# Turning the convolved values in 32x32 squares on VectorE, and one decay factor moved to POOL, in a hybrid DeltaNet and attention layer

## The chip, the cores and the metric

The kernel runs on one core of a Trainium2 chip. The metric is the device time in microseconds (us), the median of several executions. The engines are called as the profile calls them: PE (TensorE), DVE (VectorE), ACT (ScalarE), POOL (GpSimd) and SP (SyncE, whose queue issues most DMAs). PSUM holds what PE writes, SBUF is the on-chip memory, and tensors "spilled" go to device memory.

## What is computed

One layer over 2048 latent tokens and 256 context tokens of width 1024. Inputs are normed and modulated, then projected by `w_in`. Branch A is a gated DeltaNet of 4 heads, run forward and backward over the tokens; branch B is windowed attention. The part that matters here is the input of branch A:

```python
def _gdn_inputs(qkv_raw, beta_raw, decay_raw, conv_w, a_log, dt_bias):
    qkv = jax.nn.silu(_short_conv(qkv_raw, conv_w))          # 5 taps along the tokens
    q, k, v = jnp.split(qkv, [GDN_HEADS * GDN_DK, 2 * GDN_HEADS * GDN_DK], axis=-1)
    ...
    g = -jnp.exp(a_log) * jax.nn.softplus(decay_raw.reshape(b, l, 2, GDN_HEADS) + dt_bias)
# later, in chunks of tokens, for each direction:
gc = jnp.cumsum(to_chunks(g), axis=-1)
decay = jnp.where(incl, jnp.exp(jnp.where(incl, gc[..., :, None] - gc[..., None, :], 0.0)), 0.0)
```

So the values `v` of four heads (128 wide each) come out of a convolution along tokens and a SiLU, and a matrix of exponentiated decay differences is made for each 128 tokens, head and direction.

## The kernel before

The layer is worked in stages, and PE goes from one to the next without a break in the program: normed inputs and attention keys (to about 150 us), then the DeltaNet's values (`ORDER` 8 to 11, one head each), its keys (4 to 7), its queries (0 to 3), the gates, the chunk inverses, the scan over chunks, attention, and the output products.

`qkv` takes one head of one kind at a time. The tokens are cut into five segments: 256 of context and four of 512. For each segment `fm_dense` (L583 to L588) makes 24 matmuls into one of three PSUM buffers `lps`; ACT copies it to `y` (L696; four buffers); `conv` runs the five taps, the first on ACT (L623), four on DVE (L625), then a tanh on ACT (L626) and the closing product on DVE (L627). The result `cacc` has the head's 128 channels on the partitions and the tokens along the row. `finish` then puts it away. For values it was: PE transposes each 128 tokens into PSUM (L657, `zt`), ACT copies the four to `st` (L675), and one DMA stores `st`, tokens on the partitions, into `vsp` (L648, through `spill`), from where the scan loads it again (L1146).

Beside each of the first 18 segments runs one step of `all_decays`, the decay matrix of one 128-token chunk. `g` has been split into a high part `ghi` and a low part `glo`; for each direction and part, a tile `gm` = part times a 0/1 mask (`le` or `ge`) is made, and PE sums the four products of `gm` with a constant matrix in `dps` (L204). The four factors are made on different engines: number 0 (forward, high) on POOL, 1 (forward, low) and 2 (backward, high) on DVE, all by L202; 3 (backward, low) on ACT by four instructions (L200). ACT then takes the exponential (L207) and issues the store into `Dsp` itself.

Buffers matter in two places. The tile named `st` is a ring of two buffers, and factor 3 of the decays sits in the same ring; so within a head the ring is taken in this order: segment 0's `st`, `gm`, `gm`, segment 1's `st`, `gm`, segment 2's `st`, `gm`, segment 3's and segment 4's `st`, `gm`. Each taker waits until the one two before it is done with the buffer, for an `st` that means until its store has landed. Factors 0 and 1 share two buffers of their own. Values, keys and queries all use the ring `st`.

The order of instructions on every engine is set ahead of time by a scheduler that runs over a timeline of its own; each engine then runs its list strictly in order.

Of the kernel before, what the change touches and what calls it, by code (L numbers as in the profile page):

```python
# [7 lines left out]
F32 = mybir.dt.float32  # L8
# [12 lines left out]
H = 4  # L21
# [7 lines left out]
def f32(ap):  # L29
    return ap.bitcast(F32)  # L30
# [10 lines left out]
def _hybrid(ctx, tc, nc, V, S, G, T, ins, out, dbg, upto):  # L41
    dma = nc.sync.dma_start
# [5 lines left out]
    def dscr(name, shape, dt=F32):  # L48
        return dram.tile(shape, dt, name=name)
# [32 lines left out]
    g = pers.tile([128, NC, 8], F32, name="g")  # L82
# [9 lines left out]
    ksp = dscr("ksp", [NC, 128, H, 128])  # L92
    vsp = dscr("vsp", [NC, 128, H, 128])
# [49 lines left out]
    def psum(tag, shape, dt=F32, name=None):  # L143
        _, p, banks = pst["left" if tag in pst["left"][2] else "right"]
        return p.tile(shape, dt, name=name or tag, tag=tag, bufs=banks[tag])
# [44 lines left out]
    def decays(pool, matr, c, le, ge):  # L190


        dps = psum("gps", [128, H, 128], name="dps")
        n = 0
        for d, m in ((0, le), (1, ge)):
            for gx in (ghi, glo):
                gm = (pool.tile([128, H, 128], F32R, name="gm", bufs=2) if n < 2 else pb.tile([128, H, 128], F32R, name="gm", tag="dtl", bufs=1) if n == 2 else pb.tile([128, H, 128], F32R, name="gm", tag="st"))
                if n == 3:
                    for h in range(H):
                        S.activation(gm[:, h], m, AF.Copy, scale=f32(gx)[:, c, d * 4 + h:d * 4 + h + 1])  # L200
                else:
                    (G, V, V)[n].tensor_tensor(gm, f32(gx)[:, c, d * 4:d * 4 + 4].unsqueeze(2).to_broadcast([128, H, 128]),  # L202
                                               m.unsqueeze(1).to_broadcast([128, H, 128]), op=ALU.mult)
                T.matmul(dps, lhsT=matr[:, d], rhs=gm, start=n == 0, stop=n == 3)  # L204
                n += 1
        dt = pb.tile([128, H, 128], F32, name="dt", tag="o")
        S.activation(dt, dps, AF.Exp)  # L207
        adma(Dsp[c], dt)
# [41 lines left out]
    if True:  # L250
# [283 lines left out]
        for gi in range(8):  # L534
            xts = []
            for j in range(2):
                c = NCB + gi * 2 + j
# [13 lines left out]
            c = NCB + gi * 2  # L551
# [62 lines left out]
    pb = pb_.__enter__()  # L614
# [15 lines left out]
    def decay_of(h, c0, nn):  # L630
        dt = pb.tile([128, 4, 128], F32, name="dtl", bufs=1)[:, :nn]
        dma(dt, Dsp[c0:c0 + nn, :, h].rearrange("c p i -> p c i"))
        return dt

    def spill_blocks(d, t, c0, nn, h):

        for b in range(2):
            r = slice(b * 64, b * 64 + 64)
            dma(Nsp[d][c0:c0 + nn, h, b].rearrange("c r i -> r c i"), t[r, :, r])
        dma(offsp[d][c0:c0 + nn, :, h].rearrange("c r i -> r c i"), t[64:128, :, 0:64])  # L640

    def finish(m, z, c0, n):

        h = m % 4
        nn = n // 128
        b0 = c0 - NCB
        zc = [z[:, j * 128:(j + 1) * 128] for j in range(nn)]
        spill = lambda dst, t: dma(dst.rearrange("c p d -> p c d"), t)  # L648
        if m < 4:
            dma(qTsp[h, :, b0 * 128:b0 * 128 + n], z)  # L650
            kT = pb.tile([128, 4, 128], F32, name="kTl", tag="st")
            dma(kT, kTsp[h, :, c0 * 128:c0 * 128 + n].rearrange("p (c t) -> p c t", t=128))
        elif m < 8:
            dma(kTsp[h, :, c0 * 128:c0 * 128 + n], z)
        ps = psum("zt", [128, 4, 128])
        for j in range(nn):
            T.transpose(ps[:, j], zc[j], ident)  # L657
        if m < 8:
            dt = decay_of(h, c0, nn)
            for j in range(nn):  # L660
                junk = pb.tile([128, 128], BF16, name="junk", bufs=1)
                dst = ssk[:, c0 + j, h:h + 1] if m >= 4 else alpha[:, b0 + j, h:h + 1]
                S.activation(junk, ps[:, j], AF.Square, accum_out=dst)
            gps = psum("gps", [128, 4, 128])
            for j in range(nn):
                T.matmul(gps[:, j], lhsT=zc[j] if m >= 4 else kT[:, j], rhs=zc[j], start=True, stop=True)
            p = pb.tile([128, 4, 128], F32, name="p", tag="o")[:, :nn]
            V.tensor_tensor(p, gps[:, :nn], dt, op=ALU.mult)
            if m >= 4:
                spill_blocks(1, p, c0, nn, h)  # L670
            else:
                spill(QDsp[b0:b0 + nn][:, :, h], p)
        if m >= 4:
            st = pb.tile([128, 4, 128], F32, name="st")[:, :nn]
            S.copy(st, ps[:, :nn])  # L675
            spill((ksp if m < 8 else vsp)[c0:c0 + nn, :, h], st)
        if 4 <= m < 8:
            pps = psum("gps", [128, 4, 128])
            for j in range(nn):
                T.transpose(pps[:, j], p[:, j], ident)  # L680
            pt = pb.tile([128, 4, 128], F32, name="pt", tag="o")[:, :nn]
            S.copy(pt, pps[:, :nn])
            spill_blocks(0, pt, c0, nn, h)

    def qkv(order, after, w=None, beside=()):
        w = w or weights(w_in[:, order[0] * 128:order[0] * 128 + 128], KT)
        beside = iter(beside)
        for mi, m in enumerate(order):
# [3 lines left out]
            for si, (xh, xl, c0, n) in enumerate(segs):  # L692
                ps = acc([128, 512], name="lps")[:, :n]
                fm_dense(ps, w, xh, xl)
                y = py.tile([128, 516], F32, name="y", bufs=4)
                S.copy(y[:, 2:2 + n], ps)  # L696
                if c0 <= NCB:
                    V.memset(y[:, 0:2], 0.0)
                else:
                    V.tensor_copy(y[:, 0:2], ys[-1][0][:, 512:514])  # L700
                    V.tensor_copy(ys[-1][0][:, 514:516], y[:, 2:4])
                if c0 == 0 or c0 == NCB + 12:
                    V.memset(y[:, n + 2:n + 4], 0.0)
                ys.append((y, c0, n))
                if si == 1:
                    nxt = order[mi + 1] if mi + 1 < len(order) else after
                    wnext = None if nxt is None else weights(w_in[:, nxt * 128:nxt * 128 + 128], KT)
                if si == len(segs) - 1:
                    w = wnext
                    done = [ys[-2], ys[-1]]  # L710
                elif c0 > NCB or c0 == 0:
                    done = [ys[-1 if c0 == 0 else -2]]
                else:
                    done = []
                for y_, c_, n_ in done:
                    finish(m, conv(y_, m, n_), c_, n_)
                next(beside, None)
# [15 lines left out]
    def all_decays():  # L733
        matr = ev.tile([128, 4, 128], F32R, name="matr", tag="rt")[:, 0:2]
        V.tensor_copy(matr, mats[:, 2:4])
        scalars1()
        for c in range(NC):
            decays(dc, matr, c, le, ge)
            yield
# [942 lines left out]
```

## Time and profile before

| | us |
|---|---|
| median of 3 runs | 1963.31 (1960.19 to 1971.19) |
| the profiled execution | 1973.82 |
| its span, first to last instruction | 1972.1 |
| PE busy | 1910.1 |
| DVE busy | 1477.4 |
| ACT busy | 815.9 |
| POOL busy | 657.4 |

The profile is of one execution. PE, PEld (its weight loads), DVE, ACT and POOL are rows of busy time; an engine's list in order of time gives start, length and what it waited for just before. A group's row ends with "busy, mean ns of one | idle before, releaser".

### The profile page before, as it was taken

How to read it: one execution, taken by the hardware profiler on the slowest of the kernel's cores; microseconds unless marked ns; L12 is line 12 of the kernel's file. 1: busy time of each engine (PE TensorE's matmuls, PEld its weight loads, DVE VectorE, ACT ScalarE, POOL GpSimd, SP SyncE). 2: the span in 40 equal slices, each digit the busy share in tenths (PEclk: the TensorE clock that was granted, in tenths of full speed). 3: DMA queues.
4: the chain of work that ended last, by engine and by line, in shares of the span. 5: the costliest groups of instructions: out<-in, count | busy, mean ns of one | idle time of the engine just before them, and what ended most of it. 6: DMA issues, size and time to landing. Idle time of an engine off the chain costs nothing. (4 is left out here: it accounts for less than half of the span.)

```text
span 1972.1 us, 32045 instructions
## 1 busy us (share of the span) xinstructions
PE 1910.1 (97%) x10943; PEld 1606.0 (81%) x10943; DVE 1477.4 (75%) x2853; ACT 815.9 (41%) x2008; POOL 657.4 (33%) x750
## 2 busy tenths in 40 slices
PE   6899999989999999999999999999999999999999
PEld 3888888778998787887888888888878887878787
DVE  7889766677776999999778767544787777757864
ACT  6865545554444322211122233324675555532321
POOL 2652111235543201104222334422555444430353
PEclk9999999999999999999999999999999999999999
DMA  7553226765546633537887777755555555448362
GB/s 267 162 154 94 86 89 160 188 163 168 155 149 162 188 106 115 152 93 211 226 243 224 225 217 228 205 157 183 173 164 168 172 164 171 137 120 283 123 224 86
DMA packets 385463, 333.12 MB, mean 169 GB/s; under 512 B 83800, under 2 KB 307344, under 8 KB 384660
## 3 DMA queue, kind: packets, MB, share of 16 engines
q1 hardware_dynamic: 366292, 295.40, 51.7%
q10 hardware_dynamic: 19008, 35.67, 4.9%
q8 instruction: 87, 1.43, 0.3%
q14 instruction: 76, 0.62, 0.1%
HBM read 220.28 MB, written 109.13 MB: 167 GB/s over the span
## 5 line engine op out<-in xcount | busy, mean ns | idle before, releaser
L586 PE MATMUL rps<-hh,wh 128*128 128x512 f32 x768 | 309.8, 403 | 4.3 <-DVE rt L880 3.2
L587 PE MATMUL rps<-hl,wh 128*128 128x512 f32 x768 | 308.3, 401 | 0.0
L588 PE MATMUL rps<-hh,wl 128*128 128x512 f32 x768 | 307.2, 400 | 0.0
L625 DVE SCALAR_TENSOR_TENSOR cacc<-y,cw,cacc 128x512 f32<-128x512 f32 (+1 forms) x224 | 165.0, 758 | 21.1 <-ACT cacc L623 18.8
L586 PEld LDWEIGHTS rps<-hh,wh 128*128 128x128 f32 x768 | 145.4, 189 | 39.8 <-DVE rt L880 3.7
L588 PE MATMUL lps<-hh,wl 128*128 128x512 f32 (+1 forms) x448 | 171.7, 383 | 1.2 <-DVE wl L244 1.2
L586 PE MATMUL lps<-hh,wh 128*128 128x512 f32 (+1 forms) x448 | 172.0, 384 | 0.8 <-POOL wh L243 0.6
L588 PEld LDWEIGHTS rps<-hh,wl 128*128 128x128 f32 x768 | 145.3, 189 | 32.7
L587 PEld LDWEIGHTS rps<-hl,wh 128*128 128x128 f32 x768 | 145.7, 190 | 31.8
L587 PE MATMUL lps<-hl,wh 128*128 128x512 f32 (+1 forms) x448 | 171.0, 382 | 0.0
L1006 DVE TENSOR_TENSOR pl<-pt,ph 128x512 fp32r<-128x512 f32 x156 | 105.5, 685 | 45.8 <-ACT ph L1004 44.9
L1004 ACT CAST ph<-pt 128x512 fp32r<-128x512 f32 x156 | 90.6, 585 | 110.7 <-PE pt L1002 72.1
L878 ACT ACTIVATE rt<-rps 128x512 f32<-128x512 f32 x96 | 57.2, 596 | 185.1 <-PE rps L588 168.2
L978 DVE CUSTOM_DVE_ANT_0 pr<-sc,band,sk 128x640 f32<-128x640 f32 (+1 forms) x128 | 106.7, 862 | 19.9 <-PE sc L974 12.7
L811 DVE TENSOR_TENSOR N<-N,btmp 128x62 f32<-128x62 f32 (+30 forms) x124 | 118.1, 953 | 3.0
L988 POOL TENSOR_SCALAR pr<-pr,sm 128x640 f32<-128x640 f32 (+1 forms) x128 | 101.0, 809 | 55.8 <-DVE sm L986 40.3
L809 DVE TENSOR_TENSOR btmp<-N 128x62 f32<-128x62 f32 (+30 forms) x124 | 115.8, 934 | 3.1
L980 ACT ACTIVATE pr<-pr,sm 128x640 f32<-128x640 f32 (+1 forms) x128 | 104.0, 815 | 24.6 <-DVE sm L978 20.9
L244 DVE TENSOR_TENSOR wl<-wr,wh 128x512 fp32r<-128x512 f32 x120 | 90.8, 768 | 24.1 <-POOL wh L243 21.2
L1293 PE MATMUL pps<-yh,wph 128*128 128x512 f32 x256 | 105.7, 415 | 2.1 <-DVE tb L1304 2.0
L243 POOL TENSOR_SCALAR wh<-wr 128x512 fp32r<-128x512 f32 x72 | 50.3, 711 | 159.4 <-PE lps L587 57.2
L1295 PE MATMUL pps<-yh,wpl 128*128 128x512 f32 x256 | 101.9, 399 | 1.2 <-POOL wpl L1255 1.2
(396 smaller groups left out, 4961.4 us busy)
## 6 DMA issues: line engine op xcount, KB each, us to landing
wr<-in_w_in_dram SPq DMA_DIRECT2D x120, 256.0 KB
kw<-Ksp SPq DMA_DIRECT2D x28, 384.0 KB
x<-vsp SPq DMA_DIRECT2D x36, 256.0 KB
k<-ksp SPq DMA_DIRECT2D x34, 256.0 KB
kT<-kTsp SPq DMA_DIRECT2D x34, 256.0 KB
wm<-in_w_mod_dram SPq DMA_DIRECT2D x16, 512.0 KB
xt<-in_x_dram SPq DMA_DIRECT2D x16, 512.0 KB
dtl<-Dsp SPq DMA_DIRECT2D x32, 256.0 KB
```

The lines of the kernel that those rows point to most:

```text
L586: T.matmul(ps, lhsT=wh[:, k], rhs=xh[:, k], start=k == 0, stop=False)
L587: T.matmul(ps, lhsT=wh[:, k], rhs=xl[:, k], start=False, stop=False)
L588: T.matmul(ps, lhsT=wl[:, k], rhs=xh[:, k], start=False, stop=k == kt - 1)
L625: V.scalar_tensor_tensor(a, y[:, t:t + n], cw[:, m, t:t + 1], a, op0=ALU.mult, op1=ALU.add)
L809: V.tensor_tensor(tv, A[:, m + 1:, m].unsqueeze(2).to_broadcast([h1 + n, r, m]), A[:, m, 0:m].unsqueeze(1).to_broadcast([h1 + n, r, m]), o ...
L811: V.tensor_tensor(A[:, m + 1:, 0:m], A[:, m + 1:, 0:m], tv, op=ALU.add)
L978: V.tensor_tensor_reduce(s_, ps[:, o:768], band[:, b0:b0 + W + 256], -0.125, sk[:, 1, hd:hd + 1], ALU.add, ALU.min, sm[:, h, 1:2])
L980: S.activation(s_, s_, AF.Exp, scale=-1.0, bias=sm[:, h, 1:2], accum_out=sm[:, h, 2:3])
L988: G.tensor_scalar(p[:, h, :W + 256], p[:, h, :W + 256], sm[:, h, 3:4], 1.0, op0=ALU.mult, op1=ALU.mult)
L1006: V.tensor_tensor(pl, pt, f32(ph), op=ALU.subtract)
L1293: T.matmul(ps, lhsT=wh[:, k, ms], rhs=hs[k], start=k == 0, stop=False)
L1295: T.matmul(ps, lhsT=wl[:, k, ms], rhs=hs[k], start=False, stop=k == 3)
```

## The change

Two edits.

1. `finish` for values no longer uses PE, PSUM or ACT. DVE turns `cacc` by one instruction that transposes every 32x32 square in its place, straight into `st`. A partition of `st` then holds a token's place within 32, and the four groups of 32 partitions hold the four groups of 32 channels. Four DMAs, one for each group of partitions, put the squares where they belong in `vsp`, in runs of 32 numbers (128 bytes) where the one store of before had runs of 128 (512 bytes). What stands in `vsp` is the same.
2. Factor 1 of the decays (forward, low part) is made by POOL and not by DVE.

```diff
--- before.py
+++ after.py
@@ -199,7 +199,7 @@
                     for h in range(H):
                         S.activation(gm[:, h], m, AF.Copy, scale=f32(gx)[:, c, d * 4 + h:d * 4 + h + 1])
                 else:
-                    (G, V, V)[n].tensor_tensor(gm, f32(gx)[:, c, d * 4:d * 4 + 4].unsqueeze(2).to_broadcast([128, H, 128]),
+                    (G, G, V)[n].tensor_tensor(gm, f32(gx)[:, c, d * 4:d * 4 + 4].unsqueeze(2).to_broadcast([128, H, 128]),
                                                m.unsqueeze(1).to_broadcast([128, H, 128]), op=ALU.mult)
                 T.matmul(dps, lhsT=matr[:, d], rhs=gm, start=n == 0, stop=n == 3)
                 n += 1
@@ -652,6 +652,13 @@
             dma(kT, kTsp[h, :, c0 * 128:c0 * 128 + n].rearrange("p (c t) -> p c t", t=128))
         elif m < 8:
             dma(kTsp[h, :, c0 * 128:c0 * 128 + n], z)
+        if m >= 8:
+            st = pb.tile([128, 4, 128], F32, name="st")[:, :nn]
+            V.transpose(st, z.rearrange("p (c t) -> p c t", t=128))
+            for g in range(4):
+                dma(vsp[c0:c0 + nn, :, h, g * 32:g * 32 + 32].rearrange("c (k a) d -> a (c k) d", a=32),
+                    st[g * 32:g * 32 + 32].rearrange("a c (k d) -> a (c k) d", d=32))
+            return
         ps = psum("zt", [128, 4, 128])
         for j in range(nn):
             T.transpose(ps[:, j], zc[j], ident)
@@ -673,7 +680,7 @@
         if m >= 4:
             st = pb.tile([128, 4, 128], F32, name="st")[:, :nn]
             S.copy(st, ps[:, :nn])
-            spill((ksp if m < 8 else vsp)[c0:c0 + nn, :, h], st)
+            spill(ksp[c0:c0 + nn, :, h], st)
         if 4 <= m < 8:
             pps = psum("gps", [128, 4, 128])
             for j in range(nn):
```

Lines behind the new branch stand seven lines lower in the changed kernel (L675 is now L682, L696 is L703).

The scheduler sets a new order for everything from about the start of the values to the end of the queries; from the gates on the lists of the engines are the same as before. Three places show it. First PE, at the end of the context segment of a head (`zt` holds the turned values, `dps` the decay sums, `lps` the segment). Before:

```order
L586 MATMUL lps<-hh_412,wh 128x256
L587 MATMUL lps<-hl_413,wh 128x256
L588 MATMUL lps<-hh_412,wl 128x256
L657 MATMUL zt<-ident,cacc 128x128 x4
L204 MATMUL dps<-gm,matr 128x512
L586 MATMUL lps<-hh_412,wh 128x256
```

Now:

```order
L588 MATMUL lps<-hh_412,wl 128x256
L586 MATMUL lps<-hh_412,wh 128x256
L204 MATMUL dps<-gm,matr 128x512
L587 MATMUL lps<-hl_413,wh 128x256
L588 MATMUL lps<-hh_412,wl 128x256
```

The transposes are gone from the list in the values' part of the program; the matmuls of the decays stay, three together and one apart.

Second POOL, at the start of the values (`wh` is the high part of the next head's weights). Before:

```order
L243 TENSOR_SCALAR wh<-wr 128x512 x2
L202 TENSOR_TENSOR gm<-ghi,mats 128x512 x2
L243 TENSOR_SCALAR wh<-wr 128x512 x2
L202 TENSOR_TENSOR gm<-ghi,mats 128x512 x5
L243 TENSOR_SCALAR wh<-wr 128x512 x2
```

Now:

```order
L243 TENSOR_SCALAR wh<-wr 128x512 x2
L202 TENSOR_TENSOR gm<-ghi,mats 128x512
L202 TENSOR_TENSOR gm<-glo,mats 128x512
L202 TENSOR_TENSOR gm<-ghi,mats 128x512
L243 TENSOR_SCALAR wh<-wr 128x512 x2
L202 TENSOR_TENSOR gm<-glo,mats 128x512
L202 TENSOR_TENSOR gm<-ghi,mats 128x512
L202 TENSOR_TENSOR gm<-glo,mats 128x512
L202 TENSOR_TENSOR gm<-ghi,mats 128x512
L202 TENSOR_TENSOR gm<-glo,mats 128x512
```

Each decay step now has two products on POOL, the high and the low part of the forward direction; the weights' split stands between them.

Third, DVE in the middle of the second head, where the store of one segment's values and the transpose of the next meet in the ring. The list now has:

```order
L657 STREAM_TRANSPOSE st<-cacc 128x512
L705 MEMSET y 128x2
L625 SCALAR_TENSOR_TENSOR cacc<-y,cw,cacc 128x512 x2
L202 TENSOR_TENSOR gm<-ghi,mats 128x512
L625 SCALAR_TENSOR_TENSOR cacc<-y,cw,cacc 128x512
L657 STREAM_TRANSPOSE st<-cacc 128x512
L625 SCALAR_TENSOR_TENSOR cacc<-y,cw,cacc 128x512 x2
L627 SCALAR_TENSOR_TENSOR cacc<-y,cacc 128x512
L625 SCALAR_TENSOR_TENSOR cacc<-y,cw,cacc 128x512
L707 COPY y<-y 128x2
L625 SCALAR_TENSOR_TENSOR cacc<-y,cw,cacc 128x512
```

The first transpose is segment 1's and the next segment 2's. They use the same buffer, since the `gm` in between takes the other one; between them stand three convolution steps and one decay factor. DVE had no instruction on `st` before.

The queue of SP in the second to fourth head, before:

```order
L648 DMA vsp<-st 128x2x128
L239 DMA wr<-in_w_in_dram 128x4x128 x2
L648 DMA vsp<-st 128x4x128 x4
L239 DMA wr<-in_w_in_dram 128x4x128
L648 DMA vsp<-st 128x2x128
L239 DMA wr<-in_w_in_dram 128x4x128
L648 DMA vsp<-st 128x4x128 x4
L648 DMA vsp<-st 128x2x128
L239 DMA wr<-in_w_in_dram 128x4x128 x2
```

Now:

```order
L659 DMA vsp<-st 32x8x32 x4
L239 DMA wr<-in_w_in_dram 128x4x128 x2
L659 DMA vsp<-st 32x16x32 x16
L659 DMA vsp<-st 32x8x32 x4
L239 DMA wr<-in_w_in_dram 128x4x128 x2
L659 DMA vsp<-st 32x16x32 x16
L659 DMA vsp<-st 32x8x32 x4
L659 DMA vsp<-st 32x16x32 x4
L239 DMA wr<-in_w_in_dram 128x4x128 x2
L659 DMA vsp<-st 32x16x32 x4
```

Each store of before is four, in the same places among the loads of weights (`wr`).

## The prediction

> **What bounds the kernel now.** I read the page's busy row first, then the busy time by stretch, where the values are 150 to 290 us, the keys 290 to 440 and the queries 440 to 640 (columns: stretch and length; then busy us and instructions of PE, PEld, DVE, ACT and POOL; granted clock, DMA share, GB/s).
>
> ```profile
> PE 1910.1 (97%) x10943; PEld 1606.0 (81%) x10943; DVE 1477.4 (75%) x2853; ACT 815.9 (41%) x2008; POOL 657.4 (33%) x750
> 150.00:290.00 140.00, 140.00 (x698) 116.35 (x697) 111.47 (x195) 76.18 (x173) 28.88 (x28) 1.00 0.30 92
> 290.00:440.00 150.00, 141.50 (x854) 120.96 (x853) 100.28 (x203) 78.28 (x258) 31.64 (x31) 1.00 0.65 165
> 440.00:640.00 200.00, 198.56 (x1336) 179.16 (x1336) 145.82 (x333) 88.87 (x270) 90.61 (x105) 1.00 0.55 160
> ```
>
> The values stretch is the changed one, and there PE has no gap at all at full clock. DVE works 111.5 of 140 us, so 28.5 are free. What is taken from PE there shortens the stretch, one for one, as long as nothing else becomes late. In the keys and queries PE has 8.5 and 1.4 us of gaps.
>
> **The change on PE.** A stretch of PE's list shows what one set of transposes costs (start, length, instruction):
>
> ```profile
> 169.11 0.39 PE L586 MATMUL lps<-hh,wh 128*128 128x512 f32 x1
> 169.34 0.60 PE L657 MATMUL zt<-ident,cacc 128*128 128x128 f32 x4
> 169.70 0.48 PE L587 MATMUL lps<-hl,wh 128*128 128x512 f32 x1
> 170.02 0.39 PE L588 MATMUL lps<-hh,wl 128*128 128x512 f32 x1
> L657 PE MATMUL zt<-ident,cacc 128*128 128x128 f32 x72 | 11.1, 272 | 0.0
> ```
>
> Matmuls overlap, so starts count, not lengths. Two 512-wide matmuls in a row start 0.23 apart (169.11 to 169.34). From the four transposes' start to that of L588 there are 0.68 us, where one matmul alone would need 0.23: four transposes cost 0.45. In all there are 72 in the values (last row, the group of this stretch): 18 sets of four would be **8.1 us**. Nothing is put on PE. The decays' 72 matmuls stay.
>
> **ACT** loses its 20 copies (L675, 10.8 us, and the waits ahead of them). It is not the bound, but the waits stood in front of first taps that DVE needs:
>
> ```profile
> L675 ACT COPY st<-zt 128x512 f32<-128x512 f32 (+1 forms) x20 | 10.8, 542 | 21.7 <-PE zt L657 20.3 <-DMA vsp<-st 1.5
> DVE cacc L625 <- ACT cacc L623: 15.2, 6, 4.9
> ```
>
> ACT sat 20.3 us waiting for the transposes, and DVE in its turn sat 15.2 us waiting for ACT's first tap, up to 4.9 at once. Of DVE's idle time this is over half, and it should shrink. It gives DVE room; it gives the end nothing by itself, since PE has no gap there.
>
> **The change on DVE.** Three rows of DVE and one of POOL in the values stretch:
>
> ```profile
> L202 DVE TENSOR_TENSOR gm<-glo,mats 128x512 fp32r<-128x512 f32 x18 | 17.0, 944 | 8.1 <-PE dps L204 8.1
> L202 DVE TENSOR_TENSOR gm<-ghi,mats 128x512 fp32r<-128x512 f32 x18 | 12.3, 682 | 0.2 <-PE dps L204 0.2
> L625 DVE SCALAR_TENSOR_TENSOR cacc<-y,cw,cacc 128x512 f32<-128x512 f32 x68 | 53.7, 825 | 9.6 <-ACT cacc L623 9.1
> L202 POOL TENSOR_TENSOR gm<-ghi,mats 128x512 fp32r<-128x512 f32 x18 | 20.9, 1162 | 80.2 <-PE dps L204 68.9 <-DMA Ksp<-ks 11.3
> ```
>
> Moved away: 18 factors of 0.68 undisturbed (the `ghi` row), 12.3 us. Added: 16 transposes of 128x512 and 4 of 128x256. The trace has no such instruction. From below I bound it by one pass over 512 numbers, the `ghi` row's 0.68, from above by two passes, 1.36. I take one (half for the small ones), since the two 512-wide rows here, of different operations, lie close together: 16 x 0.68 + 4 x 0.34 = 12.2, and at most 24.5. So DVE's own work stays as it is, -0.1 us, or grows by 12.
>
> POOL gets 18 more products. It has room (28.9 of 140 us), but it disturbs DVE:
>
> ```profile
> 161.42 0.68 DVE L202 TENSOR_TENSOR gm<-ghi,mats 128x512 fp32r<-128x512 f32 x1
> 162.05 1.50 DVE L625 SCALAR_TENSOR_TENSOR cacc<-y,cw,cacc 128x512 f32<-128x512 f32 x1
> 161.85 1.16 POOL L202 TENSOR_TENSOR gm<-ghi,mats 128x512 fp32r<-128x512 f32 x1 [0.89 <-PE dps L204]
> 167.28 0.68 DVE L202 TENSOR_TENSOR gm<-ghi,mats 128x512 fp32r<-128x512 f32 x1
> 167.89 1.51 DVE L625 SCALAR_TENSOR_TENSOR cacc<-y,cw,cacc 128x512 f32<-128x512 f32 x1
> 169.44 0.75 DVE L625 SCALAR_TENSOR_TENSOR cacc<-y,cw,cacc 128x512 f32<-128x512 f32 x1
> 167.50 1.35 POOL L202 TENSOR_TENSOR gm<-ghi,mats 128x512 fp32r<-128x512 f32 x1 [4.50 <-PE dps L204]
> ```
>
> A convolution step takes 0.75 alone and 1.50 while POOL makes a factor, 0.76 more. Over the stretch the loss is less, for some of POOL's work falls into DVE's gaps: the `glo` factors lie 0.262 x 18 = 4.7 us above the `ghi` ones, the 68 steps 0.075 x 68 = 5.1 above 0.75; 9.8 us for POOL's 28 instructions in these two groups, 0.35 each, and with the smaller groups about 0.5, my estimate. Eighteen more: 9 us; at the least 0, at the most 18 x 1.16 = 20.9.
>
> The Trainium skill, "SBUF — State Buffer", section "Who interferes with whom", says that a DVE instruction with two inputs in SBUF and a GpSimd instruction that reads SBUF exclude each other, the later one waiting for the whole of the earlier. The two pairs above agree in kind; the stretch's mean is less. [...] The transpose has one input and by that section would not be stopped.
>
> **The stores and the ring.** Each store becomes four. What an issue, a landing and a packet cost:
>
> ```profile
> L648 SPq DMA_DIRECT2D vsp<-st x20: 359/360/458, 154.5 to 283.9; - x20
> L1058 SPq DMA_DIRECT2D x<-X4sp x32: 573/610/1251, 1212.3 to 1271.5; - x32
> 182.25 0.59 ACT L675 COPY st<-zt 128x512 f32<-128x512 f32 x1 [0.76 <-PE zt L657]
> 185.85 0.38 ACT L675 COPY st<-zt 128x256 f32<-128x256 f32 x1 [0.55 <-DMA vsp<-st]
> DMA packets 417, 0.21 MB, mean 103 GB/s; under 512 B 16, under 2 KB 417, under 8 KB 417
> q1 hardware_dynamic: 417, 0.21, 38.2%
> DMA packets 207, 0.05 MB, mean 49 GB/s; under 512 B 207, under 2 KB 207, under 8 KB 207
> q1 hardware_dynamic: 207, 0.05, 26.3%
> DMA packets 376, 0.02 MB, mean 23 GB/s; under 512 B 376, under 2 KB 376, under 8 KB 376
> q1 hardware_dynamic: 376, 0.02, 22.7%
> ```
>
> The old store was done 3.0 us after the copy (182.84 to 185.85). The packet rows are three short windows: 512-byte stores of `vsp` in 2 us (0.382 x 16 x 2 / 417 = 29 ns each), 256-byte stores of `Nsp` in 1 us (20 ns), 64-byte loads of `X4sp` in 1 us (10 ns). Between them a 128-byte packet is about 13 ns; at worst as much as a 512-byte one, 29. A set of four stores has 2048 packets: 1.7 us on 16 engines (3.7 at worst) where 512 took 1.0. DMA is at a share of 0.30 here, so room is not the matter; the landing is. Issues of patterns cut like these cost 0.61 (`X4sp` row), plain ones 0.36: the fourth goes out 1.1 to 1.8 us later than one alone, which gives 4.1 to 4.8 us behind the transpose if the packets keep up; where packets are slower than the issues it is 3.0 - 1.0 + their time, 5.7 at 29 ns. I take 4.5, between 4.1 and 6.
>
> Behind the stores on SP wait the loads of weights, at most two us longer. They are early by far more: POOL, which splits them, waits for PE to free the buffers, not for the load. The same list of waits has POOL early with the decays too, by 68.9 / 17 = 4.1 us a step, so a second product of 1.16 fits before PE needs it.
>
> ```profile
> POOL gm L202 <- PE dps L204: 68.9, 17, 8.5
> POOL wh L243 <- PE lps L587: 34.1, 5, 20.2
> ```
>
> The Trainium skill, "DMA: Bandwidth & Descriptors", section "Specifications", puts line rate at 512 bytes and more, with a read-modify-write below. The 256-byte row shows no such step (20 ns against 29), but no run here shows 128-byte stores.
>
> Now DVE waits where ACT did: a transpose waits for the store that last held its buffer, and the convolution steps behind it on DVE wait too, then `y`, the `lps` buffers and PE. I went through DVE's new list at 0.67 a step (162.05's neighbours start so), 0.6 for other 512-wide ones, half for 256, and added 0.5 to 0.7 for POOL. Between two transposes of one buffer there are, head by head, about 5.2, 4.6 and 4.3 us in the first, 3.1, 5.2 and 2.8 in the second, 3.1, 5.2 and 3.6 in the third, 4.4 and 3.5 in the last. At 4.5 us the waits add up to 1.4 + 1.7 + 1.4 + 0.9 + 1.0 and some tenths, near 7 us; at 6 us to 21; below 3 to almost nothing.
>
> **The sum.** DVE: 111.5 - 0.1 + 9 + 7 = 127 us. PE: 140 - 8.1 = 131.9. DVE still fits, but at 96%, and PE waits in order for factor 2 of the decays, which stands behind those waits on DVE. I give back 3 of the 8.1. The keys and queries have a new order with the same work; I leave their 9.9 us of gaps as they are. So -5 us: the profiled execution, 1973.82 (its span 1972.1 and 1.7 around), would be 1968.8. It lies 10.5 above the median of the runs, 1963.3, which becomes **1958 us**; this case's own range is 1954 to 1963. A measurement of this kernel tells 0.5%, 9.8 us, from no change.
>
> **Rivals.**
>
> *DVE takes PE's place.* POOL's added products stop DVE for all of their length: 111.5 - 0.1 + 20.9 = 132.3 before any wait for the ring. PE is then paced by DVE, the 8.1 are given back: 1961 to 1967, 1964. For it: the two pairs above. Against it: the mean over the stretch, and the part of DVE's 15.2 us that goes with ACT's copies. The page on SBUF has the rule.
>
> *Slower: the stores hold the ring.* If a set of four lands 7 us after the transpose and not 4.5, the gaps above leave 21 + 11 = 32 us of waits on DVE, 111.5 + 9 + 32 = 152.5 against 140: 12.5 longer, 1976. It decides from 6 us on, where the gain is gone (111.5 + 9 + 21 = 141.5). For it: four issues, four times the packets, and a DVE that stands still in order. Against it: 7 us need packets of 39 ns (3.0 - 1.0 + 2048 x 0.039 / 16), above every row. The page on DMA has the rule that could do it.
>
> *Gain on both sides.* The reordered keys also lose gaps. They had 8.5, of which 6.1 stood ahead of L680:
>
> ```profile
> L680 PE MATMUL gps<-ident,p 128*128 128x128 f32 x72 | 11.4, 277 | 6.1 <-DVE p L668 2.5 <-DVE y L698 2.1 <-DVE y L700 0.7
> ```
>
> With all 8.1 and half of these gone it is -11 to -12: 1952. For it: those waits are questions of order on DVE, which enters the keys with less behind it. Against it: nothing in the diff touches the keys, and order can add as well.
>
> **How the numbers follow.** Forecast 0.50, DVE in PE's place 0.20, slower by the ring 0.14, gain on both sides 0.16. Faster by over 0.5% (below 1953.5) is the last case and a little of the first, 0.18; slower (above 1973.1) is the ring and a little of an unlucky order, 0.16; the same 0.66. For 8 in 10 the range takes the first two cases whole and reaches into the other two: 1949 to 1971.
>
> **What would show it.** In the changed profile: L657 gone from PE and STREAM_TRANSPOSE on DVE, near 0.68 (1.36 makes DVE the bound); PE in the values without gaps ahead of L204 and L586, the stretch some 5 us shorter; L625's mean above 825 ns, by how much tells POOL's price; "DVE st waited for DMA vsp" near 7 us in the waits, and 20 or more if the ring rival holds; `glo` on POOL at 1.0 to 1.2. The prediction is wrong if the stretch is not shorter, or if the gaps of the keys move by more than a few us.

## The result

The change made the kernel slower. The changed kernel's median is 1977.02 us (1972.09 to 1980.12), against 1965.47 us (1960.19 to 1971.19) for the kernel before in the same comparison: time after / time before is **1.0054**, 95% interval 1.0041 to 1.0066. A second comparison (in the next section) gave 1.0034, 1.0017 to 1.0050 (1973.96 against 1966.81 us). One lies above the 0.5% that I had called the limit of a measurement and one below, but neither interval holds 1. The forecast was 1958, and the range ended at 1971.

The profiled execution of the changed kernel has a span of 1970.4 us and is the shortest of its seven runs, while the one of before (1972.1) is longer than all of its own; the two spans must not be subtracted. What can be compared is how far each has come at the same point of the program. I take ACT's copies of the 56 segments out of PSUM into `y` (20 of values, 20 of keys, 16 of queries). The fourth, the twentieth and the last in the list of ACT before (start, length, instruction, idle before):

```profile
152.96 0.59 ACT L696 COPY y<-lps 128x512 f32<-128x512 f32 x1 [1.55 <-PE lps L588]
...
255.26 0.57 ACT L696 COPY y<-lps 128x512 f32<-128x512 f32 x1
...
610.22 0.58 ACT L696 COPY y<-lps 128x512 f32<-128x512 f32 x1
```

And after:

```profile
152.71 0.59 ACT L703 COPY y<-lps 128x512 f32<-128x512 f32 x1 [0.89 <-PE lps L588]
...
262.30 0.57 ACT L703 COPY y<-lps 128x512 f32<-128x512 f32 x1
...
615.43 0.58 ACT L703 COPY y<-lps 128x512 f32<-128x512 f32 x1
```

From the fourth to the twentieth copy, that is in the values, it was 102.3 us and now is 109.6: **7.3 us lost where 5 were to be gained**. From the twentieth to the last, keys and queries, it was 355.0 and now is 353.1. The loss is in the stretch that the change touches; some 1.6 of the 7.3 us are matmuls that only moved there (4 more of the decays and 6 more half-wide ones between the two copies, at 0.23 and 0.12 us a start), so that from the fourth copy to the last it is 5.5 us.

The stretches of the changed kernel (columns as in the prediction) say that PE, which had no gap from 150 to 290 us, now has 10.8 us of them and a granted clock of 0.98:

```profile
150.00:290.00 140.00, 129.21 (x586) 104.47 (x585) 122.87 (x201) 68.11 (x161) 51.10 (x44) 0.98 0.40 92
290.00:440.00 150.00, 142.35 (x853) 122.39 (x853) 96.78 (x196) 76.80 (x258) 33.59 (x35) 1.00 0.67 171
440.00:640.00 200.00, 199.67 (x1357) 181.01 (x1356) 143.95 (x331) 87.10 (x258) 89.37 (x103) 1.00 0.51 153
```

Its list of waits for 150 to 290 us (engine, tile, line, what it waited for: total, times, longest) names what PE, DVE and ACT stood for:

```profile
ACT cacc L623 <- DVE st L657: 24.9, 14, 3.2
...
ACT gm L200 <- DMA vsp<-st: 11.2, 7, 2.8
PE dps L204 <- DVE gm L202: 8.6, 7, 2.6
DVE st L657 <- DMA vsp<-st: 7.4, 9, 1.5
...
DVE cacc L625 <- ACT cacc L623: 4.3, 9, 0.8
...
PE dps L204 <- DVE y L710: 2.2, 1, 2.2
```

PE's 10.8 us stand ahead of L204, the decays' matmuls. They wait for factor 2 (backward, high), the one that DVE still makes, and once for an entry behind it in DVE's list. DVE comes to factor 2 late: transposes ahead of it wait for the ring, and convolution steps are stretched while POOL works. Ahead of the longest gap (2.6 us, from 229.2) the ring took only 0.7 us of DVE's time since 215, but three pairs of steps took 2.2 to 2.35 us each, where one alone takes 0.75. ACT waits twice: its factor 3 for a store that leaves the ring (11.2 us, 6.5 before), and, new, its first tap for a transpose that still holds the `cacc` buffer (24.9). The groups of DVE and POOL in the same stretch:

```profile
L625 DVE SCALAR_TENSOR_TENSOR cacc<-y,cw,cacc 128x512 f32<-128x512 f32 x72 | 65.5, 912 | 5.3 <-ACT cacc L623 4.3
...
L202 POOL TENSOR_TENSOR gm<-glo,mats 128x512 fp32r<-128x512 f32 x18 | 21.8, 1209 | 28.0 <-PE dps L204 28.0
...
L202 DVE TENSOR_TENSOR gm<-ghi,mats 128x512 fp32r<-128x512 f32 x18 | 13.9, 774 | 0.0
...
L657 DVE STREAM_TRANSPOSE st<-cacc 128x512 f32<-128x512 f32 x16 | 11.3, 706 | 6.4 <-DMA vsp<-st 6.4
...
L657 DVE STREAM_TRANSPOSE st<-cacc 128x256 f32<-128x256 f32 x4 | 1.8, 443 | 1.0 <-DMA vsp<-st 1.0
```

A convolution step costs 912 ns in place of 825, a transpose 706 (443 at half width).

The gaps cost more than their length. Three neighbouring slices of 4 us:

```profile
226.00:230.00 4.00, 3.20 (x23) 2.67 (x22) 3.72 (x5) 0.27 (x2) 2.31 (x2) 1.00 0.00 0
230.00:234.00 4.00, 2.20 (x5) 1.81 (x6) 3.22 (x8) 1.71 (x4) 0.00 (x0) 0.70 0.28 82
234.00:238.00 4.00, 4.00 (x16) 3.14 (x16) 3.53 (x4) 2.32 (x7) 1.22 (x1) 0.87 1.02 248
```

Behind PE's longest gap the granted clock is 0.70 and 0.87. Over the 35 slices of the stretch, PE's busy time times what is missing to 1.00 comes to 2.8 us. Gaps and clock together are 13.6 us; 8.1 off that leaves +5.5, as much as from the fourth copy to the last.

### The profile page after: what moved, and what is told of

The parts are those of the page before. It is cut to its first block, busy times and chain, and to the rows that moved or that the text cites. A ratio compares the mean times of both kernels' runs of the same rounds, so it can differ in the third digit from the quotient of the medians.

```text
span 1970.4 us, 31964 instructions
## 1 busy us (share of the span) xinstructions
PE 1897.6 (96%) x10871; PEld 1594.1 (81%) x10871; DVE 1487.5 (75%) x2855; ACT 806.6 (41%) x1988; POOL 681.3 (35%) x768
## 5 line engine op out<-in xcount | busy, mean ns | idle before, releaser
L625 DVE SCALAR_TENSOR_TENSOR cacc<-y,cw,cacc 128x512 f32<-128x512 f32 (+1 forms) x224 | 172.6, 781 | 8.5 <-ACT cacc L623 5.6
L985 DVE CUSTOM_DVE_ANT_0 pr<-sc,band,sk 128x640 f32<-128x640 f32 (+1 forms) x128 | 106.7, 862 | 19.9 <-PE sc L981 12.2
L244 DVE TENSOR_TENSOR wl<-wr,wh 128x512 fp32r<-128x512 f32 x120 | 93.7, 792 | 27.6 <-POOL wh L243 24.8
L1301 PE MATMUL pps<-yl,wph 128*128 128x512 f32 x256 | 101.6, 398 | 0.0
```

Source lines behind the costliest of these rows:

```text
L625: V.scalar_tensor_tensor(a, y[:, t:t + n], cw[:, m, t:t + 1], a, op0=ALU.mult, op1=ALU.add)
L985: V.tensor_tensor_reduce(s_, ps[:, o:768], band[:, b0:b0 + W + 256], -0.125, sk[:, 1, hd:hd + 1], ALU.add, ALU.min, sm[:, h, 1:2])
L1301: T.matmul(ps, lhsT=wh[:, k, ms], rhs=ls[k], start=False, stop=False)
```

## The experiments

My theory after the result: PE loses in the values what it waits for factor 2, and DVE is late there by three things that add up: its own work, POOL's disturbance, and the ring of two `st` buffers. Rivals: POOL's disturbance alone, the stores alone, the new order of the lists alone, or something in the later stages. Where the text speaks of "gaps + clock", it is as just worked out, for 150 to 290 us; "4 to 20" and "20 to 56" are the times between these copies into `y`, "tail" the time from the last one to the end of the span.

| kernel | time / time before (95%) | gaps + clock | 4 to 20 | 20 to 56 | tail |
|---|---|---|---|---|---|
| before, first profile | | 0.0 + 0.0 | 102.3 | 355.0 | 1361.9 |
| before again | 0.9992 (0.9979 to 1.0006) | 0.0 + 0.0 | 102.3 | 353.2 | 1353.4 |
| changed, first profile | 1.0054 (1.0041 to 1.0066) | 10.8 + 2.8 | 109.6 | 353.1 | 1355.0 |
| changed again | 1.0034 (1.0017 to 1.0050) | 12.4 + 2.6 | 111.9 | 354.7 | 1357.2 |
| transposes alone | 1.0007 (0.9993 to 1.0022) | 5.4 + 1.4 | 106.5 | 350.8 | 1359.2 |
| factor 1 to POOL alone | 1.0006 (0.9994 to 1.0019) | 0.7 + 0.0 | 104.0 | 353.9 | 1363.4 |
| changed, own buffer for factor 3 | 0.9991 (0.9978 to 1.0003) | 2.9 + 0.0 | 99.7 | 350.3 | 1360.7 |
| changed, factor 2 on POOL too | 1.0050 (1.0034 to 1.0066) | 11.2 + 0.0 | 113.3 | 349.6 | 1353.0 |
| changed, one plain store | 1.0003 (0.9988 to 1.0018) | 6.5 + 3.0 | 108.7 | 344.7 | 1350.8 |
| transposes, own buffer | 0.9958 (0.9941 to 0.9974) | 1.9 + 0.0 | 97.7 | 349.0 | 1352.1 |
| the same again | 0.9959 (0.9942 to 0.9975) | 1.9 + 0.0 | 97.7 | 351.9 | 1352.0 |
| before, own buffer | 0.9991 (0.9977 to 1.0005) | 0.0 + 0.0 | 104.2 | 349.9 | 1356.6 |
| transposes, own buffer, factor 2 on ACT | 0.9945 (0.9930 to 0.9960) | 0.0 + 0.0 | 95.6 | 350.1 | 1351.8 |
| the same, factor 1 on POOL | 0.9970 (0.9959 to 0.9982) | 0.0 + 0.0 | 96.8 | 351.5 | 1353.9 |

The tail runs over the same lists in all of them and still varies by 12 us from one profiled execution to the next (8.5 between the two of the kernel before). So the times of whole kernels are taken from the ratios, and the profiles are used for the stretch. ACT copies some segments a few us late, which "4 to 20" and "20 to 56" trade against each other. And every edit lets the scheduler set a new order from the values to the queries, so no run differs from another in its edit alone; what an edit is worth is the edit together with the order that came with it.

**Both kernels again.** No edit.

> The kernel before once more, for a second profile beside the first and for the noise of the comparison. All theories: ratio 1.000 within 0.3%, median 1960 to 1970 us; PE without a gap from 150 to 290 us (140.0 of 140).

> The changed kernel once more, for a second profile. Its first profile (1972.1) is the lowest of its seven runs and loses only some 5 us by the end of the queries. Theory (PE waits in the values for factor 2 of the decays, which stands on DVE behind convolution steps, transposes and their waits; what PE saved goes into these waits and into the slower clock after them): ratio 1.004 to 1.007, about 10 us of gaps on PE ahead of L204 again and a granted clock below 1.00 behind them. Rival (the loss is in the keys and queries, by their new order alone): the values as long as or shorter than before, the keys and queries together longer by 5 us or more. Rival (the loss is in the later stages, by the clock): the gates start no later than before and the loss comes after 700 us.

Before against itself is 0.9992, so 0.15% either way is what such a comparison leaves open. The changed kernel is slower again, and by the table again in the values (9.6 us), not in the keys and queries (1.5 more than before again, 0.3 less than its first profile) and not in the tail. From the fourth copy to the last it takes 11.1 us more than before again, where gaps and clock less 8.1 make 6.9, so that account is a rough one. Its ratio lies just under the 1.004 that the theory gave as the least. The rival of later stages falls, and that of a new order in the keys and queries; the order within the values is not told apart here. Here is one wait in full. DVE in the second profile of the changed kernel, at the end of a head:

```profile
180.31 2.93 DVE L625 SCALAR_TENSOR_TENSOR cacc<-y,cw,cacc 128x256 f32<-128x256 f32 x4
183.15 0.16 DVE L708 COPY y<-y 128x2 f32<-128x2 f32 x1
183.22 0.16 DVE L707 COPY y<-y 128x2 f32<-128x2 f32 x1
185.22 0.71 DVE L657 STREAM_TRANSPOSE st<-cacc 128x512 f32<-128x512 f32 x1 [1.83 <-DMA vsp<-st]
185.85 0.38 DVE L627 SCALAR_TENSOR_TENSOR cacc<-y,cacc 128x256 f32<-128x256 f32 x1
186.16 0.68 DVE L202 TENSOR_TENSOR gm<-ghi,mats 128x512 fp32r<-128x512 f32 x1
```

and PE at that time:

```profile
184.12 0.40 PE L204 MATMUL dps<-gm,matr 128*128 128x512 f32 x1
186.89 0.79 PE L204 MATMUL dps<-gm,matr 128*128 128x512 f32 x1 [2.37 <-DVE gm L202]
187.49 0.63 PE L587 MATMUL lps<-hl,wh 128*128 128x512 f32 x1
187.91 0.63 PE L588 MATMUL lps<-hh,wl 128*128 128x512 f32 x1
188.34 0.63 PE L586 MATMUL lps<-hh,wh 128*128 128x512 f32 x1
```

The transpose stands 1.83 us for the store of an earlier one; factor 2, two places behind it, is late by that; PE waits 2.37 us with its next matmuls of `lps` ready, and then starts a matmul every 0.43 us in place of 0.23 for the next 2.5 us (187.49 to 189.99).

**Transposes alone**, factor 1 stays on DVE:

```diff
-(G, G, V)[n].tensor_tensor(gm, ...
+(G, V, V)[n].tensor_tensor(gm, ...
```

> Transposes on DVE and four stores as in the change, but factor 1 stays on DVE. DVE then has 111.5 + 11.3 = 122.8 us of work in the values before any wait, as much as the changed kernel shows (122.9), and POOL disturbs it no more than before. Theory: PE waits for factor 2 here too, 8 to 15 us in the values, and the time is as in the changed kernel, 1970 to 1980. Rival (POOL's added products alone make DVE late): L625 back at 825 ns, PE's gaps in the values under 4 us, 1958 to 1964. Rival (the stores and the ring): the transposes wait 9 us or more for the stores as in the changed kernel, and the time is within 3 us of it whatever POOL does.

None of the three came true in full. It is not as slow as the theory said (1970 to 1980, 8 to 15 us of waits for factor 2; the median is 1969.59), nor free of gaps with L625 back at 821 ns, nor do its transposes wait 9 us. The waits of 150 to 290 us:

```profile
DVE st L657 <- DMA vsp<-st: 4.9, 6, 1.6
...
PE dps L204 <- DVE gm L202: 3.7, 2, 1.9
ACT gm L200 <- DMA vsp<-st: 3.2, 4, 1.5
...
PE dps L204 <- DVE y L710: 1.5, 1, 1.5
```

Gaps and clock cost 6.8 us, about what the transposes take off PE. So half of the change has a result of nothing.

**Factor 1 to POOL alone**, values turned by PE:

```diff
-(G, V, V)[n].tensor_tensor(gm, ...
+(G, G, V)[n].tensor_tensor(gm, ...
```

> Only factor 1 goes to POOL; the values are turned by PE, copied by ACT and stored by one store as before. Theory: DVE has 111.5 - 17.0 + 10 to 17 us in the values, PE stays without gaps at 140 of 140 us and the time stays within 4 us of before (1962 to 1969). Rival (POOL's added products alone): L625 above 900 ns, gaps on PE ahead of L204, 1972 or more. Rival (the new order of keys and queries does it): the order changes here as well, and the keys and queries together lose 5 us or more with the values unchanged.

As the theory said. The disturbance is there (L625 at 923 ns), and it costs nothing that the comparison can tell, because PE hardly waits (0.7 us):

```profile
L625 DVE SCALAR_TENSOR_TENSOR cacc<-y,cw,cacc 128x512 f32<-128x512 f32 x67 | 59.6, 923 | 10.6 <-ACT cacc L623 10.2
```

The rival of POOL alone falls. Each half costs nothing by itself; together they cost 0.34 to 0.54%.

**A buffer of its own for factor 3**, so that the ring holds only turned values:

```diff
-else pb.tile([128, H, 128], F32R, name="gm", tag="st"))
+else pool.tile([128, H, 128], F32R, name="gm", tag="gm3", bufs=1))
```

> The changed kernel with factor 3 of the decays in a buffer of its own, so that the ring of two `st` buffers holds nothing but turned values. Between a transpose and the one two after it lie then 9 us or more, twice a store's landing. Theory (DVE is late for factor 2 by the sum of its work, POOL's disturbance and the 7.4 to 8.7 us that its transposes wait for the ring): these waits fall under 1.5 us, PE's gaps in the values fall from 11 to 12 us to 3 to 6 and its granted clock is 1.00 nearly throughout; ratio 0.996 to 1.000. Rival (POOL's disturbance alone): the gaps stay at 8 us or more, ratio 1.002 to 1.005. Rival (the order of the lists alone): the gaps stay and stand elsewhere.

As the theory said: the waits of DVE and ACT for `vsp` are gone from the list altogether, and of PE's there is left:

```profile
PE dps L204 <- DVE gm L202: 1.6, 3, 0.8
PE dps L204 <- ACT dt L207: 1.4, 2, 0.9
```

Nothing else was edited, though a new order came with it; L625 is even slower than in the changed kernel (934 ns against 912 and 887), and the time comes down from 1.0034 or 1.0054 to 0.9991; the intervals do not touch. The ring turned a change that would have done nothing into a loss. So did POOL's second product: without it, in the run with the transposes alone, the same ring gave 1.0007. By the ratios the own buffer is worth 0.4 to 0.6% with factor 1 on POOL and 0.5% (below) with it on DVE, and the loss needs both.

The trace of the changed kernel shows why the ring is so tight: the two buffers are not taken in turn. Factor 3 often waits for the store of the transpose just ahead of it, and so does a head's last transpose for the store of the one before, so each waits for a store that was issued a few us earlier:

```profile
162.64 0.70 DVE L657 STREAM_TRANSPOSE st<-cacc 128x512 f32<-128x512 f32 x1
166.90 1.28 ACT L200 ACTIVATE gm<-mats,glo 128x128 fp32r<-128x128 f32 x4 [2.54 <-DMA vsp<-st]
```

The description of the ring ahead of the prediction, one taker waiting for the one two before it, was wrong.

**Factor 2 on POOL too:**

```diff
-(G, G, V)[n].tensor_tensor(gm, ...
+(G, G, G)[n].tensor_tensor(gm, ...
```

> The changed kernel with factor 2 on POOL too, so that no factor stands on DVE. Theory (PE waits for factor 2 because it stands in DVE's list behind late work): the gaps of PE ahead of L204 vanish (under 2 us), DVE has 12 to 14 us less to do, POOL about 72 us in the values; some gaps of PE may come back ahead of L586 by a late `y`; ratio 0.996 to 1.001. Rival (POOL's disturbance alone): L625 goes above 950 ns, DVE gets no room, gaps of 8 us or more remain ahead of L204 or L586, ratio 1.003 or more.

A miss. L204's wait for DVE is gone, as expected, but not the gaps: PE now waits for factor 3 and for the exponential on ACT, and once 2.4 us for a late `cacc` of DVE's (at L664, in the first head of keys).

```profile
ACT gm L200 <- DMA vsp<-st: 16.0, 8, 2.7
...
PE dps L204 <- ACT gm L200: 6.3, 6, 2.1
...
DVE st L657 <- DMA vsp<-st: 5.1, 5, 1.5
...
PE dps L204 <- ACT dt L207: 2.5, 4, 1.2
```

The rival's numbers came true (11.2 us of gaps, L625 at 999 ns, 1.0050), but not only for its reason: the ring reaches PE through ACT as well. The theory had the ring on DVE alone.

**One plain store** in place of the four:

```diff
-for g in range(4):
-    dma(vsp[c0:c0 + nn, :, h, g * 32:g * 32 + 32]..., st[g * 32:g * 32 + 32]...)
+spill(vsp[c0:c0 + nn, :, h], st)
```

> The changed kernel with one plain store of `st` (runs of 512 bytes) in place of the four; it leaves out putting the squares in their places, so what stands in `vsp` is not the values. Landing should be back at about 3 us after the transpose instead of 4.6 to 5.2. Theory: the transposes' waits for the ring fall from 7.4 to 8.7 us to under 2, PE's gaps to 4 to 7 us, ratio 0.997 to 1.002. Rival (POOL's disturbance alone): gaps of 8 us or more, ratio 1.003 or more. Rival (the four stores cost by their packets, whatever waits): DMA share of the values back at 0.30 and the time below the kernel before by more than 5 us.

The DMA share is 0.31 and the ring's waits shrink: 0.7 us on DVE (7.4 to 8.7 in the changed kernel), 6.1 on ACT (11.2). The gaps fall to 6.5 us, at the theory's upper end, with three that stand at the ends of heads, one of 3.1 us:

```profile
PE dps L204 <- DVE gm L202: 6.5, 4, 3.1
...
ACT gm L200 <- DMA vsp<-st: 6.1, 5, 1.5
...
DVE st L657 <- DMA vsp<-st: 0.7, 1, 0.7
```

So the slower landing of the four stores is part of the loss, and part of PE's gaps stays without it.

**Transposes, with the own buffer, factor 1 on DVE**, twice:

```diff
-(G, G, V)[n].tensor_tensor(gm, ...
+(G, V, V)[n].tensor_tensor(gm, ...
-else pb.tile([128, H, 128], F32R, name="gm", tag="st"))
+else pool.tile([128, H, 128], F32R, name="gm", tag="gm3", bufs=1))
```

> Transposes and four stores as in the change, factor 1 back on DVE, factor 3 in a buffer of its own. Theory: without the ring's waits (4.9 us in the run with factor 1 on DVE) and without POOL's added products PE's gaps are under 3 us, most of the 8.1 us is kept: ratio 0.995 to 0.998, the fastest of these four. Rival (DVE's own work is already too much, with glo 17.0 us on it): gaps of 4 us or more, ratio 0.999 to 1.002.

> Transposes and four stores on DVE, factor 1 on DVE, factor 3 in a buffer of its own, once more, since its first timing had few runs. Theory: ratio 0.995 to 0.997, PE's gaps in the values under 3 us again. Rival (that timing was luck): 0.998 or more.

As the theory said, both times: 0.9958 and 0.9959, faster than the kernel before by 9 us. Of PE's gaps 1.9 us are left:

```profile
PE dps L204 <- DVE gm L202: 1.8, 2, 1.5
```

**The own buffer in the kernel before**, the same one line there:

> The kernel before (values turned by PE, factor 1 on DVE), with factor 3 of the decays in a buffer of its own as the only edit. Theory (the buffer removes waits on ACT and DVE only, and PE had no gap there to lose): values stretch still without gaps on PE, ratio 0.998 to 1.001. Rival (the gain of the run with transposes and the own buffer comes from the buffer and not from the transposes): ratio 0.994 to 0.997.

0.9991 (0.9977 to 1.0005): as the theory said, the buffer by itself is worth at most 0.23%, and the gain of the two runs above is not explained by it alone.

**Factor 2 on ACT**, on top of transposes and own buffer:

```diff
-if n == 3:
+if n >= 2:
     for h in range(H):
         S.activation(gm[:, h], m, AF.Copy, scale=...)
```

> As the run with transposes, factor 1 on DVE and factor 3 in a buffer of its own, and factor 2 is made by ACT as factor 3 is, by four instructions. DVE loses 18 products (14.1 us there), ACT gains 72 instructions. Theory (DVE's work at the ends of the heads is what is left of PE's gaps): the waits of L204 for DVE vanish, gaps under 1 us, ratio 0.994 to 0.997. Rival (ACT stands in order behind the convolution's tanh and becomes the late one): gaps of 4 us or more ahead of L204 waiting for ACT, ratio 0.998 or more.

As the theory said. PE has no gap again, now without the transposes on it:

```profile
150.00:290.00 140.00, 140.00 (x682) 116.25 (x680) 125.36 (x222) 97.09 (x258) 31.06 (x28) 1.00 0.47 108
```

At 0.9945 (0.9930 to 0.9960), a median of 1954.89 us, it is the fastest kernel of this study, 10.5 us below the kernel before; the intervals do not tell it from the run without this edit (0.9958).

**The same with factor 1 on POOL**, so that both edits of the change stand:

```diff
-(G, V, V)[n].tensor_tensor(gm, ...
+(G, G, V)[n].tensor_tensor(gm, ...
```

> Transposes and four stores on DVE, factor 3 in a buffer of its own, factor 2 on ACT, and factor 1 on POOL as in the change: both edits of the change stand, only the ring and factor 2 are as in the run before. Theory (POOL's second product costs where DVE is late, and DVE now makes no factor at all): L625 goes to 880 to 940 ns, DVE stays under 126 us, PE's gaps in the values under 1.5 us, ratio 0.993 to 0.997, that is within 0.2% of the run with factor 1 on DVE. Rival (POOL's disturbance costs the end by itself, 0.3% as between the two runs with the own buffer): gaps of 2 us or more, ratio 0.997 to 0.999.

Between the two. PE has no gap in the values, as the theory said, and its ratio, 0.9970, is at the edge of what that allowed; but it is 0.25% above the run with factor 1 on DVE, more than the 0.2 I had set (the two intervals just touch). 1.2 us of it stand in the values, 1.3 in keys and queries; the rest I cannot place, since the tails differ by as much from one execution to the next. The same holds for the pair with the own buffer (0.9991 against 0.9958): by the ratios POOL's second product costs 5 to 6.5 us in these two pairs, and the profiles show 0.4 to 3.3 of them up to the last copy. In the changed kernel against the transposes alone it is 0.3 to 0.5%, and in the kernel before, with PE making the transposes, 0.06%, which is within the noise.

## Why the prediction was wrong, by its own steps

- **PE**, 8.1 us off: right. With PE free of gaps on both sides, "4 to 20" is 102.3 in the kernel before and 95.6 without the transposes (factor 2 on ACT): 6.7. Of the transposes 56 of 72 fall into it, 14 sets of four, 6.3 at 0.45 each; 3 matmuls of the decays more on the one side and one half-wide matmul fewer make up some 0.6. Against the kernel before with the own buffer it is 8.6: 15 sets, 6.8, and 8 matmuls of the decays and 2 half-wide ones more, some 2.1.
- **ACT** loses its copies, and DVE's wait for the first tap shrinks: right, 15.2 to 4.3 us. What the step left out is that ACT gets other waits in their place, 24.9 us for the `cacc` that a transpose still holds (14.9 where no transpose waits for the ring), and more for factor 3's buffer, 11.2 after 6.5.
- **DVE's own work**: right. 11.3 + 1.8 = 13.1 us for the transposes against 12.2; one pass, not two.
- **POOL's disturbance**, 9 us: somewhat small. The two kernels with the own buffer differ in factor 1 and the order that came with it, and in neither does DVE wait for the ring. Their groups (512-wide convolution step, its closing product, the same two at 256, L244) differ by 0.114 x 78 + 0.064 x 18 + 0.101 x 16 + 0.281 x 4 + 0.107 x 10 = 13.9 us, 0.77 per product where I took 0.5. The product that left DVE was 787 ns there (18 of them 14.2 us). So **moving factor 1 bought DVE nothing**: from 150 to 290 us it is busy 131.8 us with factor 1 on DVE and 131.7 with it on POOL. First its groups with factor 1 on DVE, then on POOL:

```profile
L625 DVE SCALAR_TENSOR_TENSOR cacc<-y,cw,cacc 128x512 f32<-128x512 f32 x78 | 62.6, 820 | 1.5 <-ACT cacc L623 1.0
...
L202 DVE TENSOR_TENSOR gm<-glo,mats 128x512 fp32r<-128x512 f32 x18 | 14.2, 787 | 0.5 <-DMA Ksp<-ks 0.5
...
L657 DVE STREAM_TRANSPOSE st<-cacc 128x512 f32<-128x512 f32 x16 | 11.2, 702 | 0.1
```

```profile
L625 DVE SCALAR_TENSOR_TENSOR cacc<-y,cw,cacc 128x512 f32<-128x512 f32 x77 | 70.3, 934 | 1.3 <-ACT cacc L623 0.8
...
L657 DVE STREAM_TRANSPOSE st<-cacc 128x512 f32<-128x512 f32 x16 | 11.3, 703 | 0.2
```

  The Trainium skill, "SBUF — State Buffer", section "Who interferes with whom", had it in kind: the step has two inputs in SBUF and is stopped, the transpose has one and is not (702 and 703 ns). By the rule at full length the added products (24.5 us of POOL's time in the run with the own buffer) would cost all of that; they cost 13.9. Why it is less is not shown.
- **Landing and ring**: the sizes were right. In the changed kernel waiting takers of the ring start 3.6 to 5.3 us after the end of the 512-wide transpose just before them (4.5 was forecast), and DVE waits 7.4 and 8.7 us (near 7). That second size was partly luck, for it was worked out with the buffers taken in turn: 2.5 of the 7.4 us (0.97, 0.36 and 1.18) stand ahead of the last transpose of the first three heads, which by that description has another buffer than the one before it. That ACT's factor 3 waits in the same ring was in the words ahead of the prediction and in no term of its sum.
- **The sum is the step that failed**: "DVE still fits at 96%", and "I give back 3 of the 8.1". DVE's total did nearly fit (122.9 us busy and its waits, in 140), and PE lost 13.6 to 15.0 us all the same. The lateness of a factor is decided at the moment when PE comes to it, and work and waits pile up at the ends of heads, where two convolutions, two transposes and the split of the next weights meet: the three gaps of over 2 us in the changed kernel end there, at 185, 232 and 265 us. I had priced a wait by the mean of a stretch; the 3 us had no working of their own, and what they stand for measured 13.6 to 15.0. Left out were also that ACT's factor 3 could stop PE (6.3 us with three factors on POOL), and that the clock can drop behind a gap (2.6 to 2.8 us).
- **Keys and queries** "left as they are": right, 353.1 and 354.7 us against 355.0 and 353.2.
- Of the rivals, "Slower: the stores hold the ring" came nearest with 1976 and with the place of the cause, but not by its condition. It was to decide from a landing of 6 us on; it decided at 3.6 to 5.3, because the room it was measured against was the stretch's total. "DVE takes PE's place" foresaw a PE paced by DVE, at a price that ends where the gain is gone; by order, that price has no such end.

What stays open: how much of the ring's cost came through DVE and how much through ACT (only both together were taken away); where POOL's second product costs the rest of its 5 to 6.5 us; and how much of each step between two kernels is the scheduler's new order within the values and not the edit, which no run held fixed.

## What to carry to other kernels

Taking work off the bounding engine is worth its price only if what it then waits for in order is early at each step, so check the lateness at the worst place of a period (here the end of a head), not the busy share of a stretch. When a tile gets a slower way out (more or smaller stores), look up every other taker of its buffers on every engine: one buffer more, 2 KB a partition, was worth 0.4 to 0.6% where DVE made the transposes, and nothing clear of noise (0.09%) in the kernel before. And before a two-input product goes from DVE to POOL, set what it frees against what it stretches: here 14.2 us against 13.9.

## What the runs showed of the hardware that I had not expected

A short gap of PE can cost clock. Behind gaps of 2.4 us (the rows above), 2.6, 2.2, 3.1 (one plain store) and 1.9 us (transposes alone) matmuls of full width were soon 0.63 us long and started 0.43 apart, for up to some 3.5 us; in the two profiles of the changed kernel this cost 2.8 and 2.6 us. But a gap of 3.0 us in the second profile was followed by matmuls at full pace, and so were gaps of 2.1 and 2.4 us in the run with three factors on POOL and the other gap of 1.9 us in the run with transposes alone. The Trainium skill, "TensorE: Matmul & The Clock Gate", section "HAM oscillation — how this bites in real kernels", warns of gaps of more than about 3.4 us; here shorter ones were enough at times, and some nearly that long were not. What decides is not shown.

A packet of 128 bytes cost less than one of 512, but more for each byte. From 150 to 290 us the queue of these stores had, before and after (packets, MB, share of 16 engines):

```profile
q1 hardware_dynamic: 15619, 7.99, 20.6%
```

```profile
q1 hardware_dynamic: 43933, 7.98, 30.5%
```

At 0.206 x 16 x 140 / 15619 a packet of before took 30 ns. If the 9216 packets of 512 bytes that went cost that, and the other packets of the queue were the same before and after, the 36,864 of 128 bytes took (0.099 x 16 x 140 + 9216 x 0.030) / 36864 = 13.5 ns each, an estimate, close to the 13 of the prediction.
